# Two jobs on raw x: a row factor applied at PSUM eviction, and a second, normed operand built beside it

## The chip, the cores and the metric

One core of a Trainium2 chip runs the whole computation in one launch. The metric is device microseconds of that launch. Three runs of the kernel before took 1221.35, 1222.22 and 1223.20 us; the median is 1222.22 us. The engines are named as in the profile: PE (TensorE), DVE (VectorE), ACT (ScalarE), POOL (GpSimd) and SP, which issues DMAs.

## The reference, cut to what matters

Two layers of a block work on 256 tokens of 1024 channels, all in float32. What the change touches is the first norm of layer 0 and the first products behind it:

```python
def rmsnorm(x, g):
    y = x * lax.rsqrt(jnp.mean(x * x, axis=-1, keepdims=True) + EPS)
    return y * g

h = rmsnorm(x, ln_mix_pre[l])
proj = h @ w_in[l]
xr, yr, q, kv, g_nsa, qm, g_merge = jnp.split(proj, IN_OFFSETS, axis=-1)
o_a = rglru_branch(xr, yr, ...)               # xr through a convolution and a scan, yr through a gelu
o_b = nsa_branch(q, kv, g_nsa, ...)
o_c = memory_branch(qm, mem, ln_mem[l], w_mem_kv[l])   # rmsnorm(mem) @ w_mem_kv for keys and values
```

The norm has two factors: a gain per channel (g) and one number per token, the rsqrt, called the row factor here. Since it is the same for all channels of a token, `(x * g) @ w` times the row factor is the same as `h @ w`.

## The kernel before, in words

**Tiling.** Every weight matrix is cut into units of 512 KB (256 contraction rows by 512 columns as a rule). A unit is loaded into `raw` (a ring of NRAW = 5 buffers, `dma_unit`, line 334, on SP's queue), and split by `split_unit` (line 342) into a high part `whi` (ACT, a copy that rounds to fp32r) and a low part `wlo` (DVE, raw minus whi); these have rings of NSPL = 4 buffers. The operand is kept channel-major in the same two parts (`XT`, line 363: `hTh` and `hTl`, four quarters of 256 channels by 256 tokens each). Each product of two fp32 matrices is three matmuls: high by high, low by high and high by low. A job of four units (`wstat_job`, line 582) takes 96 matmuls of 256 columns into two PSUM banks.

**Order.** The jobs are issued in the order of the string ORDER0 (line 166): xr1, xr0, yr0, yr1, then vm0 (values of the memory branch), km0, and so on. `run` (line 643) issues them step by step, one step for each unit; the units are numbered u0, u1, ... here (xr1 is u0 to u3, xr0 u4 to u7, yr0 u8 to u11, yr1 u12 to u15, vm0 u16 to u19). At the top of a step it issues the splits of one or two later units, as far as `may_split` allows; then it asks `drain` for the pieces of the operand that this unit needs; then it issues the products, and after each 128 contraction rows calls `side`.

**Side work.** All that is not products lives in lanes: generators that name the engine of their next few instructions, "A", "D", "G" or "P1" (PE, with one PSUM bank to take). While the program is traced, a planner (`Order`, line 73, and `Meter`, line 106) keeps an estimated clock for every engine. `side` (line 252) goes over the lanes in the order of their priority, and within one priority in the order in which they were spawned, and issues a step if it would hold no engine up:

```python
elif r > max(od.T[e], now) + TOL or od.T[e] > now + HORIZON:   # TOL 0.07, HORIZON 3.0 us, now = od.T["P"]
    break
```

`drain` and `bank` (which waits until a PSUM bank is counted as free) call `step` (line 272) instead: it issues the step that can start first by the estimate, and of those that are within 0.3 us of each other the first in the list of lanes. The planner fixes nothing but the order; on the chip each engine then executes its instructions in that order, waiting on semaphores. The estimated PE clock knows when a unit's split is ready and which lanes are done, but a lane is done when it has been issued.

**The start.** SP loads x in four tiles (two token tiles by two halves of 512 channels), the gain as a row, and five weight units. PE runs 16 matmuls that nothing reads. `first_norm` (line 431): per token tile, ACT sums the squares of both halves, POOL adds EPS and raises to -0.5, DVE multiplies both halves by the row factor (`hn`); then per quarter PE transposes four 128x128 pieces into a PSUM bank (`tr`), ACT writes the high part with the gain as a scale per partition, and DVE the low part. Job xr1 starts with its first quarter.

At the first step `start` (line 1788) also loads the recurrent branch's gate weights, the memory's gains and the four tiles of `mem` (SP), small parameters and tables (13 DMAs on POOL's queue), and spawns in this order: the norm of `mem`, the lane `prm` (28 small DVE instructions on the recurrent parameters) and the lane `const` (the rotary tables, some 27 small DVE instructions). The norm of `mem` spawns its four half tiles (`half_lane`, line 480: DVE `hn`, PE transposes, ACT `mTh`, DVE `mTl`) only once its row factor is there, so behind prm and const in the list. vm0 needs them.

**PSUM.** Four banks tagged "mm" for products, four tagged "at" for side work. xr1's results are copied to `xs` by ACT (`xr_epi`, line 1348), which frees its two banks.

Of the kernel before, what the change touches and what calls it, by code (L numbers as in the profile page):

```python
# [11 lines left out]
F32 = mybir.dt.float32  # L12
# [60 lines left out]
class Order:  # L73
    """Estimated engine clocks, by which the issue order of independent work is chosen while it is traced."""
# [31 lines left out]
class Meter:  # L106
    """An engine whose instructions are counted on its estimated clock."""
# [38 lines left out]
def trunk_kernel(ctx, tc, x, mem, positions, ln_mix_pre, w_in, conv_w, conv_b, lru_wr, lru_br, lru_wi, lru_bi,  # L146
# [79 lines left out]
    def start_of(ln):  # L226
        """When the next instructions of this lane could start, or None while it waits for others."""
# [14 lines left out]
        if e == "V":  # L242
            ln.alt = e = min("AD", key=lambda k: max(od.T[k], ln.r + od.lat(ln, k)) + VBIAS * (k == "D"))
        r = ln.r + od.lat(ln, e)
        if len(n) > 1:
            k = int(n[1])
            if len(banks_free["at"]) < k:
                return None, e
            r = max(r, banks_free["at"][k - 1])
        return r, e  # L250

    def side():
        """Issue what can go without holding an engine up."""
# [18 lines left out]
    def step(prio=9):  # L272
        """Issues the side work of at most this priority that can start first."""
# [26 lines left out]
    def copy(dst, src):  # L300
        """On the engine that a "V" step chose."""
# [86 lines left out]
    def half_sumsq(src):  # L388
        """Sum of (src / 32)^2, a part of the mean over 1024 channels."""
# [11 lines left out]
    def first_half(src):  # L401
        """Starts the mean square of a token tile with its first half."""
# [10 lines left out]
    warm, gcol = [], []  # L413

    def load_column(g):
        """A gain as a column for every 128 channels."""
# [14 lines left out]
    def first_norm(o):  # L431
        """The first norm of x, by 256 channels of all tokens, its gain applied after the transposes."""
        hn = {}

        def scale(t):
            yield "A"
            el, box = first_half(xt[t][0])
            s1 = half_sumsq(xt[t][1])
            yield el
            yield "G"  # L440
            r = rstd_of(box[0], s1)
            for h in range(2):
                yield "D"
                hn[t, h] = a([P, 512], F32, "hn")
                dve.tensor_scalar(hn[t, h], xt[t][h], r, None, op0=OP.mult)

        def quarter(q):
            while len(hn) < NT * 2 and not all((t, q // 2) in hn for t in range(NT)):
                yield scaled
            yield "P1"  # L450
            pt = bank([P, 2, S], "at", "tr")
            for t in range(NT):
                for i in range(2):
                    c = 2 * (q % 2) + i
                    pe.transpose(pt[:, i, t * P:(t + 1) * P], hn[t, q // 2][:, c * P:(c + 1) * P], ident)
# [10 lines left out]
            for i in range(2):  # L466
                dve.scalar_tensor_tensor(o.lo[q][:, i, :], pt[:, i, :], col[i], f(o.hi[q][:, i, :]),
                                         op0=OP.mult, op1=OP.subtract)
            free()

        scaled = [spawn(scale(t), prio=0) for t in range(NT)]
        for q in range(4):
            spawn(quarter(q), f"first{q}", prio=0)

    def busy(n):
        """Products that nothing reads, to keep the tensor engine's clock up where it would wait."""
# [3 lines left out]
    def half_lane(src, r, gt, t, h, o):  # L480
        """Half a token tile, normed and transposed into channel-major parts."""
# [17 lines left out]
    def norm_lane(src, t, gt, o, name, sums=None):  # L499
        """rmsnorm of one token tile, transposed into o; the halves' lanes are name + tile + half."""  # L500
# [122 lines left out]
    def weave(js):  # L623
        """Jobs whose units take turns."""
# [18 lines left out]
    def run(jobs):  # L643
# [15 lines left out]
        def may_split(m, n):  # L659
            """Whether unit m may be split at step n."""  # L660
# [11 lines left out]
        while nd < NRAW:  # L672
            dma_unit(us[nd], 0.0)
            nd += 1
        warm.append(bank([P, 2 * P], "mm", "warm"))
# [39 lines left out]
    def epilogue(fn):  # L715
        """What follows a job's products, as urgent side work that gives its PSUM banks back."""
# [66 lines left out]
    def rope_mul(src, nh, s, t1, t2, rows=P):  # L783
        """The products of a rotation of src [rows, nh*64] in PSUM."""
# [115 lines left out]
    def gelu_lane(y, s):  # L900
        """s = 2 * gelu(y)"""
# [101 lines left out]
    def blocks_lane(l, j, g2, gx):  # L1003
        """Overlapping token blocks with their positional embedding, as contraction rows (token pair, channel)."""
# [117 lines left out]
    def kprep_lane(w, kd, res):  # L1122
        """Transposed keys of two groups times -1/8: high and low parts, each on both partition halves."""
# [17 lines left out]
    def qprep_lane(t, g, st, qs):  # L1141
        """Transposed queries of four heads: the high part on one partition half, the low part on the other."""
# [119 lines left out]
    def value_lane(l, t, g, scores, cxl, cx, ptl, st, o, before):  # L1262
        """One query tile of one group: transposed probabilities times values, all branches in one bank."""
# [16 lines left out]
        def mul(ps, vx):  # L1280
            """Rows 64*par.. of heads of parity par take the products with the high part, the other rows the low part's."""
# [34 lines left out]
    def nsa_lane(l, st, gt, o):  # L1316
        """st: q[t, g], k[g] = (hi, lo), v[br, t] = (hi, lo), c = compressed keys and values."""
# [23 lines left out]
    def layer(l):  # L1341
# [5 lines left out]
        # recurrent branch  # L1347
        def xr_epi(half):
            def go(banks):
                E["xs", half] = [a([P, 2, S], F32, "xs") for _ in range(2)]  # L1350
                yield "A"
                for b in range(2):
                    act.activation(E["xs", half][b], banks[b], AF.Copy)
# [26 lines left out]
        for half in range(2):  # L1380
            need = normed(f"bnd{l - 1}b") if l else lambda u, t: [f"first{u}"]
            J[f"xr{half}"] = wstat_job(win, 0, C_XR + 512 * half, HX, xr_epi(half), pre=pre_xr(half), unit_need=need)
            J[f"yr{half}"] = wstat_job(win, 0, C_YR + 512 * half, HX, yr_epi(half))

        # memory branch
# [31 lines left out]
        # merge  # L1417
# [414 lines left out]
```

## Time and profile before

| | us |
|---|---|
| median of three runs | 1222.22 |
| span of the profiled execution, first to last instruction | 1221.4 |
| PE busy in it | 1205.7 (99%) |
| DVE busy | 900.5 (74%) |
| ACT busy | 737.0 (60%) |
| first product of xr1 | 13.82 |
| first product of vm0 | 64.04 |

The profiled execution has no time of its own beside its span; the median lies 0.8 us above that span, which is what lies around the first and the last instruction. A matmul's end is modelled, so the distance between the starts of two matmuls is what one costs. A high part of a weight unit takes ACT about 1 us, a low part DVE 1.15 us, its 24 products take PE 2.9 us.

### The profile page before, as it was taken

The numbers are of one execution on the slowest core, as the hardware profiler recorded it, in microseconds if no ns is written. First come the engines' busy times: TensorE is split into PE (matmuls) and PEld (weight loads), VectorE is DVE, ScalarE is ACT, GpSimd is POOL, SyncE is SP. The second block draws the span as 40 slices with busy tenths as digits, with TensorE's granted clock in tenths as the row PEclk, the third lists the DMA queues.
The fourth block names the chain that finished last, engine by engine and source line by source line (L and its number), as shares of the span: only waits on it lengthen the run. The fifth ranks groups of instructions, "written<-read, shape, count | busy, mean of one in ns | idle before, by whom it ended". The sixth has DMA issues, their size and how long they took to land.

```text
span 1221.4 us, 21789 instructions
## 1 busy us (share of the span) xinstructions
PE 1205.7 (99%) x8491; PEld 1128.1 (92%) x8491; DVE 900.5 (74%) x1503; ACT 737.0 (60%) x1327; POOL 37.6 (3%) x88
## 2 busy tenths in 40 slices
PE   8999999999999999999999999999999999999997
PEld 7999988999999999998989999999999997899896
DVE  4979898968898676555567587998878867655555
ACT  5676856767666465444455688676556655645443
POOL 4000000000000020000001000000000001000000
PEclk8999999999999999999999999999999999999999
DMA  8656656644353766666657566585444356566661
GB/s 286 202 157 183 183 161 196 189 138 128 115 177 126 239 189 187 196 185 186 206 172 218 146 180 174 150 257 153 138 123 133 110 157 238 163 187 186 190 190 68
DMA packets 121271, 212.71 MB, mean 174 GB/s; under 512 B 10441, under 2 KB 24098, under 8 KB 121169
## 3 DMA queue, kind: packets, MB, share of 16 engines
q1 hardware_dynamic: 120752, 211.19, 57.0%
q8 instruction: 66, 1.08, 0.4%
q0 software_dynamic: 416, 0.15, 0.1%
q14 instruction: 37, 0.30, 0.1%
HBM read 208.16 MB, written 1.05 MB: 171 GB/s over the span
## 4 chain that ended last, share of the span: by engine, by line
PE 93%; ACT 2%; DMA 2%; DVE 2%; issue 1%; SPq 0%; POOL 0%; POOLq 0%; DVEq 0%; ACTq 0%
PE mm L140 63%; PE acc L140 14%; PE sc L140 3%; PE ob L140 2%; PE wo L140 2%; PE pt L140 2%; PE hid L140 1%; PE gp L140 1%; PE mo L140 1%; PE msc L140 1%; PE tr L140 1%; DMA mem<-in_mem_dram 1%; PE csc L140 1%; ACT junk L140 1%; DMA raw<-in_mlp_w_dram 0%
## 5 line engine op out<-in xcount | busy, mean ns | idle before, releaser
L140 DVE TENSOR_TENSOR wlo<-raw,whi 128x1024 fp32r<-128x1024 f32 (+1 forms) x371 | 447.0, 1214 | 225.3 <-ACT whi L140 224.0
L140 ACT ACTIVATE whi<-raw 128x1024 fp32r<-128x1024 f32 (+1 forms) x371 | 385.7, 1056 | 205.3 <-PE mm L140 118.8
L140 PE MATMUL mm<-hTh,whi 128*128 128x256 f32 x832 | 240.1, 289 | 0.0
L140 PE MATMUL mm<-hTh,wlo 128*128 128x256 f32 x832 | 235.8, 283 | 0.0
L140 PE MATMUL mm<-hTl,whi 128*128 128x256 f32 x832 | 235.7, 283 | 0.0
L140 PEld LDWEIGHTS mm<-hTh,whi 128*128 128x128 f32 x832 | 159.7, 192 | 1.4
L140 PEld LDWEIGHTS mm<-hTl,whi 128*128 128x128 f32 x832 | 159.8, 192 | 0.3
L140 PEld LDWEIGHTS mm<-hTh,wlo 128*128 128x128 f32 x832 | 159.8, 192 | 0.0
L140 PE MATMUL mm<-hmh,whi 128*128 128x256 f32 x480 | 135.8, 283 | 0.0
L140 PE MATMUL mm<-hmh,wlo 128*128 128x256 f32 x480 | 135.8, 283 | 0.0
L140 PE MATMUL mm<-hml,whi 128*128 128x256 f32 x480 | 135.8, 283 | 0.0
L140 PE MATMUL acc<-whi,rh 128*128 128x512 f32 x256 | 99.8, 390 | 0.0
L140 PE MATMUL acc<-wlo,rh 128*128 128x512 f32 x256 | 99.8, 390 | 0.0
L140 PE MATMUL acc<-whi,rl 128*128 128x512 f32 x256 | 99.6, 389 | 0.0
L140 PEld LDWEIGHTS mm<-hml,whi 128*128 128x128 f32 x480 | 92.1, 192 | 0.5
L140 PEld LDWEIGHTS mm<-hmh,whi 128*128 128x128 f32 x480 | 92.1, 192 | 0.5
L140 PEld LDWEIGHTS mm<-hmh,wlo 128*128 128x128 f32 x480 | 92.1, 192 | 0.0
L140 ACT ACTIVATE pr<-sc,mx 128x256 f32<-128x256 f32 (+1 forms) x128 | 52.0, 426 | 27.8 <-DVE mx L140 27.7
L140 PEld LDWEIGHTS acc<-whi,rl 128*128 128x128 f32 x256 | 48.1, 188 | 10.2
L140 PEld LDWEIGHTS acc<-wlo,rh 128*128 128x128 f32 x256 | 48.1, 188 | 9.5
L140 PEld LDWEIGHTS acc<-whi,rh 128*128 128x128 f32 x256 | 48.1, 188 | 9.5
L140 PE MATMUL mm<-whi,hTh 128*128 128x512 f32 x128 | 50.5, 394 | 0.0
(310 smaller groups left out, 2584.9 us busy)
## 6 DMA issues: line engine op xcount, KB each, us to landing
raw<-in_w_in_dram SPq DMA_DIRECT2D x136, 512.0 KB, 3.8
raw<-in_mlp_w_dram SPq DMA_DIRECT2D x128, 512.0 KB, 4.3
raw<-in_w_mem_kv_dram SPq DMA_DIRECT2D x32, 512.0 KB, 4.2
raw<-in_cmp_w_dram SPq DMA_DIRECT2D x16, 512.0 KB, 4.0
raw<-in_w_br_rnn_dram SPq DMA_DIRECT2D x16, 512.0 KB, 3.7
raw<-in_w_br_mem_dram SPq DMA_DIRECT2D x16, 512.0 KB, 3.7
raw<-in_w_br_nsa_dram SPq DMA_DIRECT2D x16, 512.0 KB, 3.7
raw<-in_w_out_dram SPq DMA_DIRECT2D x16, 512.0 KB, 4.6
```

The lines of the kernel that those rows point to most:

```text
L140: return fn(*args, **kw)
```

## The change

The diff also drops all docstrings and comments. Its core:

```diff
@@ the start: order of the loads
-    def load_x(t):
-        for h in range(2):
+    def load_x(h):
+        for t in range(NT):
             nc.sync.dma_start(out=xt[t][h], ...)
+        dma_clock[0] += 2 * 0.73
+    dma_clock[0] = 2.0
     load_x(0)
     column = load_column(ln_mix_pre[0:1, :])
-    load_x(1)
-    dma_clock[0] = 2.4 + 4 * 0.73
...
-    first_norm(env[0]["X"])
+    first_operands(env[0]["X0"], env[0]["X"])
-    run(order)
+    run(order, lambda: load_x(1))          # called behind the DMA of the first weight unit
@@ def first_operands(o, on), in place of first_norm(o)
+        ones = a([P, P], F32, "ones")
+        pool.memset(ones, 1.0)
         def quarter(q):
-            ...                             # waited for hn
             yield "P1"
-            pt = bank([P, 2, S], "at", "tr")
+            pts[q] = pt = bank([P, 2, S], "at", "tr")
-                    pe.transpose(pt[...], hn[t, q // 2][:, c * P:(c + 1) * P], ident)
+                    pe.transpose(pt[...], xt[t][q // 2][:, c * P:(c + 1) * P], ident)
             ...                             # high part (ACT, gain as scale), low part (DVE): as before
-            free()
+        def scale(t):
+            ...                             # sums of squares (ACT), rstd (POOL): as before
+            yield "D"
+            diag[t] = a([P, P], F32, "diag")
+            dve.tensor_scalar(diag[t], ident, r, None, op0=OP.mult)
+        def spread():
+            yield [spawn(scale(t)) for t in range(NT)]
+            yield "M1"                      # PE, with one "mm" bank
+            pt = bank([P, NT, P], "mm", "rs")
+            for t in range(NT):
+                pe.matmul(pt[:, t, :], ones, diag[t], start=True, stop=True)
+            rows.append(a([P, S], F32, "rows"))
+            yield "D"
+            dve.tensor_copy(rows[0], pt.rearrange("p t c -> p (t c)"))
+            free("mm")
+        def normed_quarter(q):
+            yield f"@first{q}"
+            yield "@rows"
+            n = a([P, 2, S], F32, "xn")
+            yield "D"
+            for i in range(2):
+                dve.scalar_tensor_tensor(n[:, i, :], pts[q][:, i, :], gcol[0][:, 2 * q + i:2 * q + i + 1], rows[0],
+                                         op0=OP.mult, op1=OP.mult)
             free()
+            yield "A"
+            act.activation(on.hi[q], n, AF.Copy)
+            yield "D"
+            dve.tensor_tensor(on.lo[q], n, f(on.hi[q]), op=OP.subtract)
         for q in range(4):
+            od.cur.r = 5.0 if q < 2 else 8.2
             spawn(quarter(q), f"first{q}", prio=0)
+        spawn(spread(), "rows", prio=0.2, child=0.2)
+        for q in range(4):
+            spawn(normed_quarter(q), f"norm{q}", prio=0.3)
@@ xr_epi, layer 0
+                    yield "@rows"
+                    yield "D"
+                    for b in range(2):
+                        dve.tensor_tensor(E["xs", half][b], banks[b], bc(rows[0], ...), op=OP.mult)
-                yield "A": act.activation(E["xs", half][b], banks[b], AF.Copy)     (kept for layer 1)
@@ jobs of layer 0
-            J[f"xr{half}"] = wstat_job(win, 0, C_XR + 512 * half, HX, ...)
+            J[f"xr{half}"] = wstat_job(win, 0, C_XR + 512 * half, lambda: E["X0"], ...)
+            need = None if l else lambda u, t: [f"norm{u}"]
             J[f"yr{half}"] = wstat_job(win, 0, C_YR + 512 * half, HX, yr_epi(half), unit_need=need)
```

So xr1 and xr0 multiply x times gain (operand X0, tiles xTh and xTl). The row factors of all tokens are laid out along the free axis on every partition (`rows`, from a product of a matrix of ones with two diagonal matrices), xr's results are multiplied by them on the way out of PSUM, and the normed operand X for all later jobs is built from the same transposes, whose four "at" banks are held until then. `start_of` learns the step "M1".

## Rows read from the trace of the kernel before

**Rows 1.** The page, part 1: busy us, share of the span, instructions.
```profile
PE 1205.7 (99%) x8491; PEld 1128.1 (92%) x8491; DVE 900.5 (74%) x1503; ACT 737.0 (60%) x1327; POOL 37.6 (3%) x88
```
**Rows 2.** Waits of PE, whole span: waiter, releaser: us in total, times, longest.
```profile
PE tr L140 <- DVE hn L140: 5.6, 5, 2.8
```
**Rows 3.** Timeline of the first 20 us: start, duration, engine, line, operation, count, [idle before].
```profile
2.48 3.49 PEld L140 LDWEIGHTS warm<-dmask,identr 128*128 128x128 f32 x16 [2.48 <-DVE dmask L140]
...
7.09 0.44 PE L140 MATMUL tr<-ident,hn 128*128 128x128 f32 x2 [0.67 <-DVE hn L140]
8.06 0.63 ACT L140 ACTIVATE junk<-xt 128x512 bf16<-128x512 f32 x1 [1.11 <-DMA xt<-in_x_dram]
...
11.08 0.84 ACT L140 ACTIVATE hTh<-tr,gcol 128x256 fp32r<-128x256 f32 x2 [2.29 <-PE tr L140]
...
11.95 0.88 DVE L140 SCALAR_TENSOR_TENSOR hTl<-tr,gcol,hTh 128x256 fp32r<-128x256 f32 x2 [1.26 <-ACT hTh L140]
...
12.74 2.42 DVE L140 TENSOR_TENSOR wlo<-raw,whi 128x512 fp32r<-128x512 f32 x3
...
13.82 0.41 PE L140 MATMUL mm<-hTh,whi 128*128 128x256 f32 x1
...
17.08 0.28 PE L140 MATMUL mm<-hTh,whi 128*128 128x256 f32 x1
```
**Rows 4.** DMA issues of 2.9 to 3.2 us, then of 3.2 to 3.6: us to landing (median).
```profile
raw<-in_w_in_dram SPq DMA_DIRECT2D x1, 512.0 KB, 6.4
xt<-in_x_dram SPq DMA_DIRECT2D x1, 256.0 KB, 5.5
...
raw<-in_w_in_dram SPq DMA_DIRECT2D x2, 512.0 KB, 6.8
```
**Rows 5.** Windows, PE alone: stretch, us, busy (count), granted clock, DMA share, GB/s.
```profile
9.50:9.80 0.30, 0.00 (x0) 0.67 1.06 410
...
16.30:16.60 0.30, 0.30 (x4) 0.79 1.02 389
```
**Rows 6.** Timeline of ACT, 17 to 31 us.
```profile
17.77 2.95 ACT L140 ACTIVATE whi<-raw 128x1024 fp32r<-128x1024 f32 x3
...
26.71 0.63 ACT L140 ACTIVATE junk<-mem 128x512 bf16<-128x512 f32 x1 [4.19 <-DMA mem<-in_mem_dram]
...
29.37 1.06 ACT L140 ACTIVATE xs<-mm 128x512 f32<-128x512 f32 x2
```
**Rows 7.** Timeline of DVE, 17 to 83 us.
```profile
18.86 3.50 DVE L140 TENSOR_TENSOR wlo<-raw,whi 128x1024 fp32r<-128x1024 f32 x3
...
78.88 0.69 DVE L140 TENSOR_TENSOR ml<-mm,mh 128x512 fp32r<-128x512 f32 x1 [1.24 <-ACT mh L140]
```
**Rows 8.** Timeline of SP, the issue of DMAs.
```profile
3.00 12.56 SPq L338 DMA_DIRECT2D raw<-in_w_in_dram  x7
...
17.98 4.01 SPq L1752 DMA_DIRECT2D mem<-in_mem_dram  x4
```
**Rows 9.** Timeline of PE: the seventh product of xr0, the first of vm0.
```profile
27.86 0.28 PE L140 MATMUL mm<-hTh,whi 128*128 128x256 f32 x1
...
64.04 0.40 PE L140 MATMUL mm<-whi,mTh 128*128 128x512 f32 x1
```
**Rows 10.** Timeline of DVE, 42 to 62 us: prm, half tiles of mem, const.
```profile
42.51 0.18 DVE L140 TENSOR_SCALAR sp<-sp 128x16 f32<-128x16 f32 x1
42.72 0.17 DVE L140 TENSOR_TENSOR sp<-sp,sp 128x16 f32<-128x16 f32 x1
...
44.94 1.41 DVE L140 TENSOR_TENSOR mTl<-tr,mTh 128x256 fp32r<-128x256 f32 x4
...
52.75 1.13 DVE L140 SCALAR_TENSOR_TENSOR ang<-rnd,ang 128x96 f32<-128x96 f32 x4
...
60.01 1.08 DVE L140 TENSOR_TENSOR mTl<-tr,mTh 128x256 fp32r<-128x256 f32 x3
```
**Rows 11.** Windows, all engines: stretch, us, busy of PE, PEld, DVE, ACT, POOL.
```profile
25.00:30.00 5.00, 5.00 (x44) 5.00 (x43) 0.00 (x0) 3.29 (x10) 1.51 (x6) 1.00 1.05 387
```

More of the change, by code (lines that the diff above doesn't have):

```diff
@@ L243, in start_of @@
             ln.alt = e = min("AD", key=lambda k: max(od.T[k], ln.r + od.lat(ln, k)) + VBIAS * (k == "D"))
+        tag = "at"
+        if e == "M":
+            e, tag = "P", "mm"
         r = ln.r + od.lat(ln, e)
@@ L246, in start_of @@
             k = int(n[1])
-            if len(banks_free["at"]) < k:
+            if len(banks_free[tag]) < k:
                 return None, e
-            r = max(r, banks_free["at"][k - 1])
+            r = max(r, banks_free[tag][k - 1])
         return r, e
@@ L411, in rstd_of @@
         return r
-    warm, gcol = [], []
+    warm, gcol, rows = [], [], []
     def load_column(g):
@@ L429, in load_column, with first_operands @@
         return lane()
[L431 to L441, printed above, removed]
-            for h in range(2):
-                yield "D"
-                hn[t, h] = a([P, 512], F32, "hn")
-                dve.tensor_scalar(hn[t, h], xt[t][h], r, None, op0=OP.mult)
+    def first_operands(o, on):
+        ones = a([P, P], F32, "ones")
+        pool.memset(ones, 1.0)
+        pts = {}
         def quarter(q):
-            while len(hn) < NT * 2 and not all((t, q // 2) in hn for t in range(NT)):
-                yield scaled
             yield "P1"
-            pt = bank([P, 2, S], "at", "tr")
+            pts[q] = pt = bank([P, 2, S], "at", "tr")
             for t in range(NT):
@@ L454, in quarter @@
                     c = 2 * (q % 2) + i
-                    pe.transpose(pt[:, i, t * P:(t + 1) * P], hn[t, q // 2][:, c * P:(c + 1) * P], ident)
+                    pe.transpose(pt[:, i, t * P:(t + 1) * P], xt[t][q // 2][:, c * P:(c + 1) * P], ident)
             busy(BUSY)
@@ L468, in quarter @@
                                          op0=OP.mult, op1=OP.subtract)
-            free()
-        scaled = [spawn(scale(t), prio=0) for t in range(NT)]
+        def scale(t):
+            yield "A"
+            el, box = first_half(xt[t][0])
+            s1 = half_sumsq(xt[t][1])
+            yield el
+            yield "G"
+            r = rstd_of(box[0], s1)
+            yield "D"
[19 more added lines that the diff above has]
+                                         op0=OP.mult, op1=OP.mult)
+            free()
+            yield "A"
+            act.activation(on.hi[q], n, AF.Copy)
+            yield "D"
+            dve.tensor_tensor(on.lo[q], n, f(on.hi[q]), op=OP.subtract)
+        diag = {}
         for q in range(4):
+            od.cur.r = 5.0 if q < 2 else 8.2
             spawn(quarter(q), f"first{q}", prio=0)
+        spawn(spread(), "rows", prio=0.2, child=0.2)
+        for q in range(4):
+            spawn(normed_quarter(q), f"norm{q}", prio=0.3)
     def busy(n):
@@ L641, in weave, with run @@
         return Job([js[n].units[i] for _, n, i in turns], lambda: None, mm, unit_need=unit_need)
-    def run(jobs):
+    def run(jobs, between):
         us, flat = [], []
@@ L674, in run @@
             nd += 1
+            if nd == 1:
+                between()
         warm.append(bank([P, 2 * P], "mm", "warm"))
@@ L1350, in go @@
                 E["xs", half] = [a([P, 2, S], F32, "xs") for _ in range(2)]
-                yield "A"
-                for b in range(2):
-                    act.activation(E["xs", half][b], banks[b], AF.Copy)
+                if l == 0:
+                    yield "@rows"
+                    yield "D"
+                    for b in range(2):
+                        dve.tensor_tensor(E["xs", half][b], banks[b], bc(rows[0], "p (o s) -> p o s", [P, 2, S]), op=OP.mult)
+                else:
+                    yield "A"
+                    for b in range(2):
+                        act.activation(E["xs", half][b], banks[b], AF.Copy)
                 free("mm", 2)
@@ L1381, in layer @@
             need = normed(f"bnd{l - 1}b") if l else lambda u, t: [f"first{u}"]
-            J[f"xr{half}"] = wstat_job(win, 0, C_XR + 512 * half, HX, xr_epi(half), pre=pre_xr(half), unit_need=need)
-            J[f"yr{half}"] = wstat_job(win, 0, C_YR + 512 * half, HX, yr_epi(half))
+            J[f"xr{half}"] = wstat_job(win, 0, C_XR + 512 * half, (lambda: E["X"]) if l else (lambda: E["X0"]), xr_epi(half),
+                                       pre=pre_xr(half), unit_need=need)
+            need = None if l else lambda u, t: [f"norm{u}"]
+            J[f"yr{half}"] = wstat_job(win, 0, C_YR + 512 * half, HX, yr_epi(half), unit_need=need)
         def m_epi(rnd, key):
@@ L1757, in mem_prep @@
         spawn(norm_both(ms, gm, env[l]["M"], f"mnorm{l}"))
-    def load_x(t):
-        for h in range(2):
+    def load_x(h):
+        for t in range(NT):
             nc.sync.dma_start(out=xt[t][h], in_=x[0, t * P:(t + 1) * P, 512 * h:512 * h + 512])
+        dma_clock[0] += 2 * 0.73
+    dma_clock[0] = 2.0
     load_x(0)
     column = load_column(ln_mix_pre[0:1, :])
-    load_x(1)
-    dma_clock[0] = 2.4 + 4 * 0.73
     for l in range(DEPTH):
@@ L1781, in trunk_kernel @@
                 u.early = True
-    env[0]["X"] = XT("hT")
+    env[0]["X0"], env[0]["X"] = XT("xT"), XT("hT")
     od.cur.r = 4.5
     spawn(column, "gcol", prio=0)
-    first_norm(env[0]["X"])
+    first_operands(env[0]["X0"], env[0]["X"])
     first_pre = order[0].pre
```

## The prediction

> **What bounds the kernel now.** The page's first part comes first: PE is busy for 99% of the span [rows 1], so the time moves only if products start earlier or wait more. The waits of PE come second: nearly all it waits for after its first instruction is `hn`, 5.6 us, of which the longest, 2.8 us, lies in the start [rows 2]. The timeline of the start shows why. The last tile of x lands at 8.0, its sum of squares and POOL's power follow, transposes end 11.0, the high part takes ACT 0.84, the low part DVE 0.88, the first `wlo` comes behind them, and xr1's first product stands at 13.82 [rows 3]. PE meanwhile lost its clock: the granted clock falls at about 9.6, some 2 us after the transposes that ended at 7.5, and is back at about 16.4 [rows 3, 5]; the first 12 products cost 0.21 us each and not 0.12. So 13.82 us is what the change can attack. Two more readings decide: what ACT and DVE do up to 64 us, and in which order, since both execute in the order that the planner wrote.
>
> **Part 1, the start (removes).** The first quarter no longer needs the row factor, only x's first halves, which are now the first two loads. PE's 16 matmuls end at 6.0 [rows 3], the gain column and four transposes follow to 7.0, the high part to 7.85, the low part to 8.7. The first weight unit takes the place of x's third and fourth tile, so it lands where the fourth did, 2.53 + 5.5 = 8.0 and not 3.0 + 6.4 = 9.4 [rows 4]; its first high part ends 8.6, the first `wlo` (0.6 of a group of 2.42) at 9.4. First products at 8.7, steady from 9.4: 4.4 us earlier than 13.82. PE has been idle for under 2 us, so I keep the high clock: 12 × 0.09 = 1.1 us more. x's second halves land at 9.4; the transposes of quarters 2 and 3 stand behind 12 products (10.6) and wait for nothing; were they 1.4 us late, as much as the loads were swapped by, PE would wait 0.2. The transposes themselves cost the same on x as on hn. POOL's 13 DMA issues now stand ahead of the powers; the sums they follow end after 15 anyway.
>
> **Part 2, quarter 2 (adds a wait).** Going through the planner's conditions with its own costs: at the side call in u0's step the row-factor lanes (priority 0.2) put four sums of squares on ACT ahead of quarters 2 and 3. By the estimate those high parts end at 14.3 and 14.9, their low parts could start on DVE at 14.4 while DVE's clock stands at 12.6, so they are left; the next step's splits of u2 and u3 take DVE to 18.3, over 3 us ahead of PE, and the low parts are issued behind them. On the chip: the second weight unit lands at about 10.6 (the median 6.8 of two [rows 4]), `whi` of u1 ends 11.7, quarter 1 12.4, four sums at 0.67 15.1 (from 26.71 to 29.37 [rows 6]), quarters 2 and 3 16.6, `whi` of u2 17.6, of u3 18.6; DVE then `wlo` u2 to 18.8 and u3 to 20.0 (1.15 each [rows 7]), and the first low part of quarter 2 at 20.4 (0.44 [rows 3]). PE ends u1 at 16.3 and waits about 4 us. Before, u2 began at 17.08 + 36 × 0.12 = 21.4, so 1 us of the lead is left.
>
> The clock in this wait. Before, an idle stretch of about 2 us cost the high clock [rows 3, 5]; 4 us should too. Twelve products at 0.21 were lost time of 1.1 us then; 12 to 28 now are 1.1 to 2.5. The Trainium skill (TensorE: Matmul & The Clock Gate, "HAM oscillation") says that the half rate is the default and that every wait for data long enough throttles PE anew, so that products after it start cold. The rows bear out one such fall. By that rule PE alone would reach the mark of part 3 at 28.5 to 29.9, without it at 27.4; since part 3's own wait ends at 29.8, what the rule moves is the 1.0 us for the clock in part 4: without it the forecast would be 1227.4.
>
> **Part 3, xr0's second bank (adds a wait).** Take the seventh product of xr0, at 27.86 before [rows 9], as the mark. Banks tagged "mm": one is the warm-up's, two xr1's, the fourth now holds the spread row factors (`rs`) until DVE copies them. xr0 needs two, and gets only the warm-up's; so `bank` steps until the copy is issued. But the top of that step has by then issued u6's split, and the side call before it the sums over `mem`. So DVE's copy stands behind `wlo` of u6, that behind `whi` of u6 on ACT, that behind four sums that wait for mem. Behind the waiting ACT instruction are queued all later high parts, behind DVE's the copy and xr1's eviction, and PE waits for the copy. Mem landed at 26.7 [rows 6]; SP issued it from 17.98, after two raw loads that waited for the low parts of u0 and u1 [rows 8]. Those end 2.3 us earlier now (12.9 for 15.2), and the same bytes follow, so mem comes at about 24.4 (23.4 to 25.4). Then 2.66 for the sums, 1.0 `whi`, 1.2 `wlo`, 0.4 the copy (between 0.35, a 128x256 read of PSUM in the group of four [rows 10], and 0.44 [rows 3]), and handovers: 29.8. Two fp32 products of the ones are nowhere in the trace; below, a transpose (0.2 each [rows 3]), above, the longest matmul (0.4 [rows 9]); 0.5 for both, hidden beside this wait. Mark at 29.9: **2.0 us behind** before.
>
> **Part 4, vm0's operand (moves).** DVE did nothing from 25 to 30 [rows 11]; it still waits for mem then, and afterwards has more to do. Already before, prm and const kept the half tiles of mem waiting: four `mTl` come only after prm, three only after const, at 61.1, 2.9 us before vm0 [rows 9, 10]. Before, the half tiles' `hn` were in DVE's queue ahead of prm; now DVE's estimated clock stands at its limit of 3 us ahead of PE through xr0, yr0 and yr1, each allowance goes to evictions and normed quarters, then to prm, then const, all earlier in the list, and the four `hn` are issued only by vm0's drain, behind the rest of const. DVE from 29.8 on:
>
> - evictions of xr1 and xr0, 4 × 0.65 (128x512 from PSUM: 0.69 [rows 7]) = 2.6
> - normed quarters: 8 × 0.42 = 3.4 [rows 3], 4 subtractions × 0.62 = 2.5
> - `wlo` of u7 to u18: 12 × 1.15 = 13.8
> - prm 28 × 0.21 = 5.9, const 27 × 0.25 to 0.28 = 6.8 [rows 10]
> - the wait for xr0's end (its eviction stands before `wlo` of u10): 1.5
>
> Sum 36.5: 66.3. Three `hn` (128x512, 0.69 each), transposes and the first ACT copy: vm0's products run from about 69.3. PE wants to start vm0 at 29.9 + 282 × 0.12 + 0.3 = 64.0 and idles 2 us or more until the transposes; another low-clock stretch, at vm0's start, 0 to 2 us, taken at 1.0. The end moves by 69.3 − 64.04 + 1.0 = **6.2**. The bounds: DVE's list is good to 1.5 us either way, mem's landing to 1, the clock to 1; if the half tiles get in before const, 6.8 less, and part 3 alone remains. Behind vm0 DVE lags in the recurrent branch's work, which no job reads for many units; I take 0 (0 to 2 if it delays a `wlo`). The eight more tiles of X0 and four of xn lie in a ring of 66 buffers that the first jobs don't fill: 0.
>
> Sum: span 1221.4 + 6.2 = 1227.6, with the 0.8 around it by the median 1228.4 us.
>
> **The rivals.**
> (a) The lead holds. Were low parts and copy ahead of the weights' on DVE, PE would keep the 4.4 + 1.1 less 0.5 for the added products: 1217.2. For it: PE bounds, and DVE's empty 25 to 30 could take the new work. Against: the order above, which doesn't hang on a close call except the copy's (0.13 us of estimate). Chance 0.10.
> (b) Only part 3 holds, vm0's operand comes in time: 1222.2 + 2.0 = 1224.2. For it: 2.9 us of slack before. Against: the list of 36.5 us. It decides where `hn` is issued before const. Chance 0.20.
> (c) Forecast, parts 3 and 4: 1228.4. Chance 0.55.
> (d) More: const and the recurrent branch's instructions push vm0's second half tiles too, and the low clock lasts: 3 to 5 us more, about 1232.5. Chance 0.15.
>
> **How the numbers follow.** A measurement of this kernel can tell 0.2%, 2.4 us, from no change. (a) is faster, (b) lies within, (c) and most of (d) are slower: 0.10, 0.20, 0.70. Range: (c) with its bounds is 1225 to 1231; it reaches down to cover most of (b) and up to the lower part of (d): 1222.5 to 1232.
>
> **What would show it.** xr1's first product near 9; PE idle from about 16 to 20 with DVE's `xTl` as releaser; the copy into `rows` behind a `wlo` that waits for ACT's sums over mem, and xr0's products into its second bank near 30; `mTl` after the last of const, and vm0's first product near 69. I am wrong if PE runs through from 9 to 64 without these waits, or if vm0 starts before 66.

## The result, and the profile after

The changed kernel took 1231.57 us (median of 4, 1231.26 to 1233.36), the kernel before beside it 1221.86 us: ratio 1.0074, 95% interval 1.0059 to 1.0088. Slower, as forecast (1228.4 us, 1222.5 to 1232.0), by 9.7 us where the prediction had 6.2. The profiled execution is 1231.78 us with a span of 1230.1; the span grew by 8.7. (The text ahead of the prediction puts 0.8 us outside the span; that is a median less the span of one execution. Where time and span of one execution are both on record, 1.7 to 1.9 us lie outside it for either kernel.)

TensorE's row of the page, and its waits up to 240 us (waiter, releaser: us in total, times, longest); they answer to [rows 1] and [rows 2]:
```profile
PE 1208.7 (98%) x8495; PEld 1129.5 (92%) x8495; DVE 908.5 (74%) x1518; ACT 738.3 (60%) x1327; POOL 37.0 (3%) x89
```
```profile
PE mm L140 <- DVE xTl L140: 2.9, 1, 2.9
PE mm L140 <- DVE wlo L140: 2.8, 3, 1.7
PE warm L140 <- DVE dmask L140: 2.5, 1, 2.5
PE tr L140 <- DVE hn L140: 1.9, 1, 1.9
PE gp L140 <- DVE xc L140: 1.0, 1, 1.0
PE mm L140 <- ACT whi L140: 0.7, 1, 0.7
```
The `hn` waits of the start are gone, and others have come, nearly all on VectorE. The longest, in the timelines of ACT, PE and DVE up to 30 us (start, duration, engine, operation, count, [idle before]; they answer to [rows 3, 6, 7]):
```profile
6.75 1.28 ACT L140 ACT_TABLE_LOAD   x1 [6.75 <-DVE gcol L140]
8.05 0.84 ACT L140 ACTIVATE xTh<-tr,gcol 128x256 fp32r<-128x256 f32 x2
...
22.59 0.63 ACT L140 ACTIVATE junk<-mem 128x512 bf16<-128x512 f32 x1 [2.79 <-DMA mem<-in_mem_dram]
```
```profile
20.60 0.38 PE L140 MATMUL mm<-xTl,whi 128*128 128x256 f32 x1 [2.90 <-DVE xTl L140]
...
27.80 0.61 PE L140 MATMUL rs<-diag,ones 128*128 128x128 f32 x4
...
28.96 0.35 PE L140 MATMUL mm<-xTh,whi 128*128 128x256 f32 x1
```
```profile
17.00 2.36 DVE L140 TENSOR_TENSOR wlo<-raw,whi 128x1024 fp32r<-128x1024 f32 x2 [3.56 <-ACT whi L140]
19.28 1.65 DVE L140 SCALAR_TENSOR_TENSOR xTl<-tr,gcol,xTh 128x256 fp32r<-128x256 f32 x4
...
26.33 1.23 DVE L140 TENSOR_TENSOR wlo<-raw,whi 128x1024 fp32r<-128x1024 f32 x1 [2.74 <-ACT whi L140]
28.45 0.42 DVE L140 COPY rows<-rs 128x256 f32<-128x256 f32 x1 [0.90 <-PE rs L140]
```
Quarter 2's low part stands behind two `wlo`, TensorE is idle to 20.60, and xr0's seventh product (28.96; 27.86 in [rows 9]) is 1.1 us late although the first product came 4.4 us earlier. Around vm0, DVE and PE:
```profile
64.15 0.21 DVE L140 TENSOR_SCALAR ang<-ang 128x96 f32<-128x96 f32 x1
64.27 2.07 DVE L140 SCALAR_TENSOR_TENSOR hn<-mem,rstd,gain 128x512 f32<-128x512 f32 x3
```
```profile
65.08 2.44 PE L140 MATMUL tr<-ident,hn 128*128 128x128 f32 x12 [1.85 <-DVE hn L140]
67.17 0.77 PE L140 MATMUL mm<-whi,mTh 128*128 128x512 f32 x1
...
75.84 0.67 PE L140 MATMUL gp<-xc,gw 128*128 128x256 f32 x2 [0.99 <-DVE xc L140]
...
134.06 0.38 PE L140 MATMUL mm<-mTh,wlo 128*128 128x256 f32 x1 [1.71 <-DVE wlo L140]
```
`hn` follows the last constant; vm0 starts at 67.17 (64.04 in [rows 9]). The granted clock fell about 1 us behind the end of each of the two waits (windows: stretch, us, busy (count), clock, DMA, GB/s; they answer to [rows 5]):
```profile
21.80:25.00 3.20, 3.20 (x17) 0.50 1.05 389
...
66.00:69.50 3.50, 3.50 (x14) 0.51 0.01 4
```

One table serves all that follows: when TensorE issued its first weight product, vm0's first, and the first of the compressed scores (`csc`); the us between these two; and the span. From `csc` to the end every kernel took 988.0 to 989.1 us.

| kernel | first | vm0 | csc | csc − vm0 | span |
|---|---|---|---|---|---|
| before | 13.82 | 64.04 | 233.42 | 169.4 | 1221.4 |
| changed | 9.46 | 67.17 | 241.78 | 174.6 | 1230.1 |
| e4_clock | 9.46 | 68.61 | 243.22 | 174.6 | 1231.8 |
| a_noxn | 9.46 | 67.41 | 241.86 | 174.5 | 1230.0 |
| a_xspool | 9.46 | 69.31 | 243.86 | 174.6 | 1232.1 |
| e3_mem_later | 9.46 | 66.48 | 241.03 | 174.6 | 1229.4 |
| e1_mem_first | 9.46 | 65.05 | 243.07 | 178.0 | 1231.7 |
| e5_prm_mem | 9.39 | 66.24 | 243.40 | 177.2 | 1231.8 |
| e2_low_first | 9.15 | 59.33 | 235.66 | 176.3 | 1224.6 |
| c12 | 9.46 | 60.11 | 230.01 | 169.9 | 1218.3 |
| c12t | 8.76 | 59.79 | 229.34 | 169.6 | 1218.4 |
| c_xspool | 8.46 | 61.45 | 234.64 | 173.2 | 1223.7 |
| b_load | 11.65 | 73.43 | 242.81 | 169.4 | 1230.9 |
| b_spread | 10.73 | 65.34 | 239.55 | 174.2 | 1228.4 |

Of the changed kernel's 8.7 us, 3.1 stand at vm0, 5.2 between vm0 and `csc`, and 0.3 behind.

### The profile page after: what moved, and what is told of

Same layout as the page of the kernel before. It is cut to its first block, busy times and chain, and to the rows that moved or that the text cites. A ratio compares the mean times of both kernels' runs of the same rounds, so it can differ in the third digit from the quotient of the medians.

```text
span 1230.1 us, 21818 instructions
## 1 busy us (share of the span) xinstructions
PE 1208.7 (98%) x8495; PEld 1129.5 (92%) x8495; DVE 908.5 (74%) x1518; ACT 738.3 (60%) x1327; POOL 37.0 (3%) x89
## 4 chain that ended last, share of the span: by engine, by line
PE 91%; DVE 3%; ACT 2%; DMA 1%; issue 1%; POOL 0%; SPq 0%; DVEq 0%; POOLq 0%; ACTq 0%
PE mm L140 61%; PE acc L140 14%; PE sc L140 3%; PE ob L140 2%; PE wo L140 2%; PE pt L140 2%; PE hid L140 1%; PE mo L140 1%; PE gp L140 1%; DMA raw<-in_mlp_w_dram 1%; PE tr L140 1%; PE msc L140 1%; DVE wlo L140 1%; ACT whi L140 1%; PE csc L140 1%
## 5 line engine op out<-in xcount | busy, mean ns | idle before, releaser
L140 PE MATMUL mm<-hTh,whi 128*128 128x256 f32 x768 | 221.7, 289 | 0.0
L140 PE MATMUL mm<-hTh,wlo 128*128 128x256 f32 x768 | 217.4, 283 | 0.6 <-DVE wlo L140 0.6
L140 PE MATMUL mm<-hTl,whi 128*128 128x256 f32 x768 | 217.2, 283 | 0.0
L140 PEld LDWEIGHTS mm<-hTh,whi 128*128 128x128 f32 x768 | 146.9, 191 | 1.4
L140 PEld LDWEIGHTS mm<-hTh,wlo 128*128 128x128 f32 x768 | 146.9, 191 | 0.9 <-DVE wlo L140 0.8
L140 PEld LDWEIGHTS mm<-hTl,whi 128*128 128x128 f32 x768 | 147.0, 191 | 0.3
```

Source lines behind the costliest of these rows:

```text
L140: return fn(*args, **kw)
```

## The experiments

The theory at the outset: the order costs the time (low parts, copy and half tiles of mem stand behind other work), and each misplacement that is mended pays its wait back. The rival: VectorE's added work has to be paid whatever the order.

**Half tiles of mem ahead (e1_mem_first).**
```
-        spawn(norm_both(ms, gm, env[l]["M"], f"mnorm{l}"))
+        spawn(norm_both(ms, gm, env[l]["M"], f"mnorm{l}", 1 if l else 0.35))
```


> Layer 0's half tiles of mem get a higher priority (0.35 for 1), so that their products of mem and gain (hn) are issued on VectorE ahead of the parameter and constant work; no work is added or left out, and the start stays as in the changed kernel (quarter 2's low part late, the spread copy behind wlo of u6). Theory of order: the wait of 1.85 us before the transposes of the first half tile and the low clock behind it (about 1.6 us) come from hn standing behind the constants. Then vm0's first product stands near 65.1 (64.04 before, 67.17 in the changed kernel), vm0 starts at the high clock, and the end comes 3 to 4 us earlier: about 1227.5 us. Rival, theory of load: VectorE is full from 28 to 66 us whatever the order, so that the work displaced (parameters, constants) makes the recurrent branch's xc late instead; then the waits for xc grow by what hn gives back and the time stays at 1230 to 1232 us.

Measured: 1233.09 us, ratio to before 1.0086 (1.0073 to 1.0100). vm0 started at 65.05, as the theory had it, without a wait and at full clock; and nothing was gained. The new wait stands elsewhere (timelines of PE, DVE and SP, 105 to 150 us):
```profile
130.50 0.58 PE L140 MATMUL mm<-mTh,wlo 128*128 128x256 f32 x1 [4.63 <-DVE wlo L140]
```
```profile
127.37 0.35 DVE L140 TENSOR_TENSOR gs<-g,pet 128x120 f32<-128x120 f32 x1 [5.55 <-DMA g<-kcs]
128.44 0.87 DVE L140 TENSOR_TENSOR gs<-g,pet 128x120 f32<-128x120 f32 x3 [0.71 <-DMA g<-kcs]
129.23 1.21 DVE L140 TENSOR_TENSOR wlo<-raw,whi 128x1024 fp32r<-128x1024 f32 x1
```
```profile
110.32 11.84 SPq L341 DMA_DIRECT2D raw<-in_w_mem_kv_dram  x4
122.25 0.50 SPq L1522 DMA_DIRECT2D g<-kcs  x1
```
`kcs` was written by 117.6, but its DMA to `g` stood in SP's queue behind the issue of four weight loads that took 11.84 us; VectorE's `gs` waited for that DMA, the `wlo` behind `gs`, and TensorE for the `wlo`. Both theories missed it: the rival's time (1230 to 1232) was 1.1 us short, and not through the gates' xc, for which nothing waited here.

**Parameters, then mem, then constants (e5_prm_mem).**
```
+        spawn(norm_both(ms, gm, env[l]["M"], f"mnorm{l}", 1 if l else 0.35))
+        spawn(prm_lane(prows), "prm", prio=0.33)
```


> The changed kernel with another order of priorities alone: parameters first, then the half tiles of mem, then the constants (in the run with mem first the parameters came last of the two and the gates' xc went behind; there TensorE lost 4.6 us at 126 us to wlo behind a gs that waited 5.5 us for a DMA). Theory of place: hn in time and xc not pushed, so vm0's first product at about 65 us, no wait for hn, smaller waits for xc: 1225 to 1228 us. Rival: VectorE's list between 28 and 100 us is as long as before and the order only picks who waits: 1230 to 1233 us.

Measured: 1232.70 us, 1.0081 (1.0064 to 1.0098), with `wlo` waited for 4.8 us at one place and the loads of weights ahead of `g` for 11.84 us again. So which of the two goes first doesn't matter; with the late start hn in time is worth nothing in either.

**Sums of squares behind quarter 3 (e2_low_first).**
```
         def scale(t):
+            yield "@first3"
             yield "A"
```


> One line is added: a token tile's sums of squares wait in the planner until quarter 3 has been issued. That puts the high and low parts of quarters 2 and 3 ahead of the splits of u2 and u3, and the copy of the spread row factors ahead of wlo of u6 and of the sums over mem; no work is added or left out. Theory of order: the idle 2.9 us for quarter 2's low part and its low clock go, xr0's seventh product comes at about 23.6 us (27.86 before, 28.96 in the changed kernel), VectorE starts its list some 4 us earlier, hn of mem is no longer late, and the lead of about 4 us lasts to the end: about 1218 us, faster than the kernel before. Rival, theory of load: the added VectorE work (about 8 us of normed quarters, copy and subtractions) must be paid before vm0 and the gates in any order; the lead is taken back as a wait at vm0 or at the gates, and the time is 1225 to 1230 us.

Measured: 1226.06 us, 1.0030 (1.0018 to 1.0043): 5.5 us better than the changed kernel, still slower than before. The idle 2.9 us went, TensorE was at full clock from its first product on, vm0 came at 59.33, 4.7 us ahead of before. Then 6.9 us more than before were lost up to `csc`, 4.8 of them in short waits (`wlo` 2.0 us in 3, `mTl` 1.3, `vx` 1.1, hn 0.4). The theory of order is right for the start and wrong for the end; the rival, theory of load, had the time (1225 to 1230) and the lead taken back behind vm0's start.

**Both edits (c12).** The lines of e1 and e2 together.

> Both edits of order together: the sums of squares of the token tiles wait for quarter 3, and the half tiles of mem go ahead of parameters and constants. Theory of order: the lead of the start (4.4 us and the 1.1 us for the clock, less 0.5 for the added products) lasts: 1217 to 1218 us, at most 1 us from the first edit alone, since that alone already lifts hn ahead of most of the parameter work. Rival, theory of load: 1225 us or more, with waits for the gates' xc in place of those for hn.

Measured: 1220.69 us (11 runs) beside 1222.64, ratio 0.9984 (0.9975 to 0.9993): faster than both kernels, though than the one before by less than the 0.2% set in the prediction. It lies between the two theories' bands. Apart from the 2.5 us at the very start, no wait for VectorE over 0.5 us is left up to 240 us:
```profile
PE warm L140 <- DVE dmask L140: 2.5, 1, 2.5
PE mm L140 <- DVE wlo L140: 0.5, 1, 0.5
PE mm L140 <- ACT whi L140: 0.4, 1, 0.4
PE mm L140 <- DVE vx L140: 0.3, 1, 0.3
```
The edit that gave nothing alone gives 5.4 us here: the two don't add. Where mem went first with the late start, vm0 was followed by 178.0 us; here, with the same work in another order on TensorE and VectorE, by 169.9. SP issues its DMAs in the same order in both runs; here `gs` waited 0.82 us for `g`, there 5.55.

**The low clock at vm0 (e4_clock).**
```
+        if o is env[0].get("M") and (t, h) == (0, 0):
+            for i in range(16):
+                pe.eng.matmul(pt[:, 0:2, :], identr, dmask, start=True, stop=True)
         for i in range(4):
             pe.transpose(pt[:, i, :], hn[:, i * P:(i + 1) * P], ident)
```


> The changed kernel with 16 products that nothing reads (128x256, ahead of the transposes of the first half tile of mem), in the stretch of 1.85 us in which TensorE waits for hn; every other instruction keeps its place. Theory: the first products of vm0 run at 0.43 us and not 0.22 because the engine stood idle, which costs about 1.6 us; with the wait filled the granted clock stays at 1.00 there and the end comes 1.0 to 2.0 us earlier: 1229.5 to 1230.5 us. Rival: the clock is low there for another reason, or the slow products only fill a time in which later operands would be waited for anyway (gates, wlo); then the time stays within 0.5 us of the changed kernel's 1231.6.

Measured: 1233.01 us, 1.0087 (1.0073 to 1.0101). The clock was held:
```profile
66.00:69.50 3.50, 3.48 (x24) 1.00 0.38 136
```
and nothing came of it (1.4 us above the changed kernel, outside both bands). From the spread products (`rs`, 29.59; 27.80 in the changed kernel, whose start was quicker) to vm0 it took 39.0 us instead of 39.4; then the gates waited 1.6 us for xc instead of 1.0. Up to `csc` TensorE waited 4.0 us for 3.3 and was 0.7 us quicker with its products: vm0's slow products had filled a time that was waited for anyway.

**VectorE without xn (a_noxn).**
```
-                dve.scalar_tensor_tensor(n[:, i, :], pts[q][:, i, :], ..., rows[0], ...)
+            nc.gpsimd.memset(n, 0.5)
+                od.note("D", ...)
```


> The changed kernel, every engine's order as it is, without VectorE's eight products of quarter, gain and row factor (xn, 8 x 0.47 us); the tile that they fill is set to a constant by POOL, so the normed operand's values are left out. Theory of load (VectorE has more to do between 28 and 78 us than it has time for): what VectorE loses TensorE gets back, hn of mem comes 3.3 us earlier, the wait of 1.9 us and its low clock go, the waits for xc and wlo behind it shrink, and the time falls by 3 to 5 us to 1227 to 1228.5 us. Rival, theory of place: the late instructions wait for a DMA, for ScalarE or for the planner's place whatever VectorE's load, so that the wait only moves and the time stays within 1 us of 1231.6.

Measured: 1232.43 us, 1.0087 (1.0072 to 1.0101): no gain. VectorE did 3.3 us less, and `hn` still started at 64.88:
```profile
40.00 1.41 DVE L140 TENSOR_TENSOR xs<-mm,rows 128x512 f32<-128x512 f32 x2 [2.94 <-PE mm L140]
```
Its queue came to xr0's eviction, which the change moved from ScalarE to VectorE, and stood there 2.94 us until TensorE had ended xr0. In the changed kernel that wait is 1.47 us, and the eviction starts at 39.40; what is saved ahead of it is waited there. From this eviction to `hn` it took 24.9 us in both kernels. So VectorE's list of instructions before vm0 is dated from the end of xr0, not from the copy. In this run the clock stayed at 1.00 from 64 to 72 us, with the same wait of 1.85 us, and `csc` was the same.

**xr's eviction off VectorE (a_xspool).**
```
-                    yield "@rows"
-                    yield "D"
-                        dve.tensor_tensor(E["xs", half][b], banks[b], bc(rows[0], ...), op=OP.mult)
+                    yield "A"
+                        act.activation(raw[b], banks[b], AF.Copy)
+                    free("mm", 2)
+                    yield "@rows"
+                    yield "G"
+                        pool.tensor_tensor(E["xs", half][b], raw[b], bc(rows[0], ...), op=OP.mult)
```


> The changed kernel; the results of xr1 and xr0 leave PSUM as plain copies on ScalarE (as before the change), and POOL multiplies them by the row factors from SBUF. Nothing is left out. VectorE loses its four products of 0.69 us and, with them, the place in its queue at 38.6 us where it waits 1.5 us for xr0's last product; half tiles of mem stay behind the constants. Theory of the queue (what stands behind xr0's eviction on VectorE is dated from xr0's end, so that eight fewer xn gave nothing): hn comes about 4 us earlier (60 for 64.3), the wait of 1.9 us goes, xc comes earlier too and the waits for xc and wlo behind vm0 (3.3 us) shrink: 1224.5 to 1227.5 us. Rival: the next wlo waits for ScalarE and so for TensorE in its place, and takes the time up as in the run without xn: over 1230 us.

Measured: 1233.34 us, 1.0083 (1.0067 to 1.0100); `hn` at 66.42. VectorE's list, from the copy (32.41) to `hn`, ran without the wait for xr0, in 34.0 us for 35.8. It should have been 4.3 shorter (1.5 and 2.8), but POOL's products slowed it:
```profile
34.44 2.17 DVE L140 TENSOR_TENSOR wlo<-raw,whi 128x1024 fp32r<-128x1024 f32 x1
...
43.09 0.96 DVE L140 TENSOR_SCALAR hb<-pcol 128x32 f32<-128x32 f32 x1
43.97 0.16 DVE L140 TENSOR_SCALAR sp<-pcol 128x16 f32<-128x16 f32 x1
44.16 1.15 DVE L140 TENSOR_TENSOR sp<-sp,pcol 128x16 f32<-128x16 f32 x1
```
```profile
32.97 2.56 POOL L140 TENSOR_TENSOR xs<-xu,rows 128x512 f32<-128x512 f32 x2 [6.14 <-DVE rows L140]
41.71 3.57 POOL L140 TENSOR_TENSOR xs<-xu,rows 128x512 f32<-128x512 f32 x2 [6.18 <-ACT xu L140]
```
2.17 for 1.21, 0.96 for 0.18 and 1.15 for 0.17: 2.7 us given back. And the copy itself came 4 us later than in the changed kernel: it stands behind `wlo` of u6 in both, but `whi` of u6 now stood behind ScalarE's copies of xr1, which waited 3.12 us for TensorE. The run can't tell the theory from its rival cleanly; what it shows is that this way out costs as much as it saves.

**Sums over mem later (e3_mem_later, one run).**
```
-        od.cur.r = max(od.cur.r, dma_clock[0] + 2.0)
+        od.cur.r = max(od.cur.r, dma_clock[0] + 2.0) + (0 if l else 4.0)
```


> The changed kernel with layer 0's sums over mem allowed 4 us later in the planner, so that whi of u6 stands ahead of them on ScalarE; quarter 2's low part stays late. If the sums over mem price xr0's start, as the prediction's third part has it, TensorE's wait of 0.7 us for whi goes and xr0's seventh product comes 0.7 to 1.5 us earlier than 28.96. Rival: TensorE's own late restart at 20.6 us prices it, and the product stays within 0.3 us. hn of mem stays behind the constants either way, so the time is 1230 to 1232 us in both.

Measured: 1231.38 us. `whi` of u6 now stood ahead of the sums, and waited 5.06 us for TensorE to give a buffer back; xr0's seventh product came at 29.16. The rival holds: TensorE's own restart prices that mark, the sums over mem don't. (The wait of 0.7 us for `whi` that the theory counted on stands at 9.46, ahead of the first product, and not at xr0's start: from 20.60 to 28.96 the changed kernel's TensorE waits for nothing.)
```profile
25.04 1.06 ACT L140 ACTIVATE whi<-raw 128x1024 fp32r<-128x1024 f32 x1 [5.06 <-PE mm L140]
26.01 0.61 ACT L140 ACTIVATE junk<-mem 128x512 bf16<-128x512 f32 x1
```

**The added work on the kernel before (b_load, b_spread).**
```
+            for _ in range(k):   # k by unit: b_load u6 to u9 4, 4, 3, 3; b_spread u10 to u16 2 each
+                nc.vector.tensor_tensor(scr, xt[0][0], xt[0][1], op=OP.subtract)
```


> The kernel before, every engine's order as it is, with 14 subtractions of 128x512 that nothing reads on VectorE behind wlo of u6 to u9 (4, 4, 3, 3; about 0.65 us each, 9.1 us in all): the size of the work that the change adds to VectorE, without any of the change's start. Theory of load: VectorE stood idle for 4.9 us between 28 and 64 us, so that some 4 us are left over; vm0 or the gates wait for them and the time rises by 3 to 6 us. Rival: the cost of the change lies in the late low part of quarter 2 and in the order, and the added work finds room: less than 1.5 us.

> The kernel before, every engine's order as it is, with the same 14 subtractions of 128x512 that nothing reads, now two behind each wlo of u10 to u16 (42 to 61 us), behind the half tiles' hn. In this stretch VectorE of the kernel before shows no idle time, and its last mTl ends 2.9 us before vm0. Theory of the list (each us added there moves everything behind it, and 2.9 us of it are slack): vm0 about 6 us later, 1227.5 to 1229.5 us. Rival (wlo run ahead of TensorE by the ring of buffers, so that added work is caught up): under 2.5 us.

Measured: b_load 1232.63 us, 1.0085 (1.0071 to 1.0100); b_spread 1230.20 us, 1.0056 (1.0038 to 1.0075). Both cost more than either theory gave: 10 us for 10.0 us of work (14 × 0.71), and 8. In b_load four stand ahead of the first two hn in VectorE's queue and four ahead of the other two, and TensorE has mem's transposes in its own queue there:
```profile
33.01 2.86 DVE L363 TENSOR_TENSOR scr<-xt,xt 128x512 f32<-128x512 f32 x4
35.79 0.74 DVE L140 SCALAR_TENSOR_TENSOR hn<-mem,rstd,gain 128x512 f32<-128x512 f32 x1
```
```profile
36.58 1.12 PE L140 MATMUL tr<-ident,hn 128*128 128x128 f32 x4 [6.00 <-DVE hn L140]
```
All of it is lost at vm0 (9.4), nothing behind (169.4). b_spread is the reverse: vm0 only 1.3 later, 4.8 lost behind it (2.6 more in waits, 2.2 in slow products behind the longest of them). The order on every queue is that of the kernel before in both; what differs is how far VectorE is when TensorE starts vm0. The first xc for the gates starts 3.0 us ahead of vm0's first product in the kernel before, 2.4 ahead in b_load, and 3.3 behind in b_spread (2.4 behind in the changed kernel). The lines are of before, b_spread and b_spread:
```profile
61.00 1.51 DVE L140 SCALAR_TENSOR_TENSOR xc<-xs,pcol,xc 128x255 f32<-128x255 f32 x3
```
```profile
68.67 1.51 DVE L140 SCALAR_TENSOR_TENSOR xc<-xs,pcol,xc 128x255 f32<-128x255 f32 x3
```
```profile
71.38 0.50 PE L140 MATMUL mm<-wlo,mTh 128*128 128x512 f32 x1 [1.99 <-DVE wlo L140]
```
Two of the subtractions added in b_spread, 1.4 us, run behind vm0's start. So VectorE of the kernel before had no room for 10.0 us of work in either place; the changed kernel's VectorE is busy 8.0 us more (908.5 for 900.5).

**The table load, and the version with it (c12t, c_xspool).** In c12t, one line on c12; c_xspool is c12t with the edit of a_xspool.
```
+    early = cp.tile([P, 1], F32, name="early")
+    nc.scalar.activation(early, mhalf, AF.Copy)
```


> The kernel with both edits of order, and one more: a 128x1 copy on ScalarE at the start, whose only use is that the table load of 1.28 us, which stood behind the gain column at 6.75 us, comes before it. Theory: the first high part stands behind the table load, so the first product comes 0.8 to 1.3 us earlier (8.2 to 8.7 for 9.46), and the end about 1 us: 1219.7 for 1220.7 us. Rival: the first weight unit's landing and its split set the steady start, or VectorE's list sets vm0 anyway; then the first product moves and the time does not.

> The version with both edits of order and the early table load, with xr's results through ScalarE and POOL as in the first of these runs. If VectorE's list is still what limits the lead behind xr0, the end comes 0.5 to 1.5 us earlier than the 1220.8 us of that version; if not (no wait for VectorE stands in its trace from 30 to 120 us), it stays within 0.7 us of it.

Measured: c12t 1220.80 us, 0.9987 (0.9978 to 0.9996). The table load went to 0.79, the first product came at 8.76 and `csc` 0.7 us earlier; the time is that of c12. c_xspool 1223.74 us, 1.0007 (0.9997 to 1.0017): 2.9 us worse than c12t, where the forecast was better or the same, with 4.1 us of waits for `wlo` behind the start. c12 and c12t are the versions to keep; they can't be told apart.

## Why the prediction came out as it did

The direction and the cause (in-order queues on VectorE, as the planner wrote them) were right, and the time lies 3.2 us above the forecast. That is above forecast (c)'s own bounds (1225 to 1231) and where rival (d) stood (3 to 5 us more), but not by (d)'s mechanism: the fourth half tile's `hn` did come only behind vm0's start (68.91), but no wait of 0.3 us for it shows in the changed kernel, and the low clock's price was nil. That the range still held the time is in part luck, since two terms were too large and a third was missing. Of its signs one didn't come as said: vm0 at 67.17, not near 69. By its steps:

- **Part 1.** First products at 9.46 and not 8.7, steady from 10.45 and not 9.4: the table load, at 0.79 us before the change, now stands behind the gain column, at 6.75, for 1.28 us (0.7 of the 0.76 us, by c12t). That was not seen. The clock was at its high level from the first product, as said.
- **Part 2.** Right: TensorE waited for quarter 2's low part until 20.60 (20.4 forecast), 2.9 us and not 4 since it came there later, and the clock stood at 0.50 until 25. e2_low_first, which mends it and also puts the copy of part 3 ahead, shows that the start is worth the most: 5.5 us alone, 10.9 with mem's order.
- **Part 3.** The order came as walked, copy behind `wlo` of u6 behind the sums over mem, but it priced nothing: mem landed at 22.59, not 24.4, and VectorE waited 0.90 for TensorE's `rs`, not TensorE for it. The mark was 1.1 us late, not 2.0, all of it from part 2 (e3_mem_later).
- **Part 4.** Right in kind: hn behind the last constant, at 64.27. The list was put at 36.5 us from 29.8 and took 35.4 from 28.87, so vm0 came 3.1 us late and not 5.2. The term of 1.5 for xr0's end was in the sum; that work saved ahead of it therefore brings `hn` no earlier (a_noxn) was not seen.
- **The clock, 1.0.** It fell at vm0 to 0.51, but its price was nil (e4_clock, a_noxn). The Trainium skill (TensorE: Matmul & The Clock Gate, "HAM oscillation") has every wait that is long enough throttle the engine anew. The rows at vm0 don't settle whether 1.85 us is long enough: that wait was followed by 0.51 in the changed kernel and by 1.00 in a_noxn. In neither did it change the end.
- **Behind vm0, 0 to 2.** The step that failed. It cost 5.2 us. Its ground was that no job reads the recurrent branch's work for many units; TensorE's gates (`gp`) come 7.1 us after vm0's first product, and waited for xc. Five kernels with the changed kernel's order on every queue from vm0 on lost 5.2 to within 0.2, though their vm0 lay anywhere from 66.5 to 69.3, with the low clock or without: it isn't how late vm0 is. In all five xc also starts 2.4 to 2.6 us behind vm0's first product, and b_spread lost 4.8 in the order of the kernel before, with xc 3.3 behind. So VectorE's lag at vm0 can cost nearly as much by itself. The order counts too: c12, where the gates come 16.7 us after vm0's first product, lost only 0.5 with xc 5.5 behind. How much of the 5.2 is the lag and how much the changed kernel's order, no run separates. Named in the trace are the gates' xc (1.0 to 1.6 us), and `wlo`, 0.6 and 1.3 to 1.7; that last stands behind `gs`, which waited 3.1 us for the DMA of `kcs`. In the changed kernel 1.9 us of the 5.2 are no wait: about 1 is vm0's slow products (the first six start 67.17 to 69.45), 0.4 the fourth half tile's transposes, which stood ahead of vm0 before; for the rest there is only the other order. What makes the planner write that order was not tried.
```profile
72.42 0.60 PE L140 MATMUL tr<-ident,hn 128*128 128x128 f32 x4
```

Measured, 3.1 + 0 + 5.2 against 5.2 + 1.0 + 0: two terms too large, one missed. Behind `csc` another 0.3 was lost, and the 0.8 us that the sum adds outside the span is 1.7 in the changed kernel's profiled execution: the profiled execution of before, with a span of 1221.4, was longer than most (the median span of the other runs is 1220.6 to 1220.9). Rival (a), the lead holds, put at 1217.2 if the low parts and the copy went first: with the order mended (c12) 1220.69. vm0 was then 3.9 us ahead, not 5.0, and the start of the kernel before was less of a loss than its profile shows. In b_load and b_spread, the same instructions up to there, x's last tile was read at 6.7 and 6.6 and not 8.06 [rows 3], and the first product stood at 11.65 and 10.73; b_spread then waited 2.1 us for hn of mem, up to 31.8, where the kernel before waited 0.2: half of its earlier start (1.6 of 3.1 us) was given back there.

## What to carry to other kernels

Ask of an edit that shifts a written order not only which wait it removes, but which instructions change places on each in-order queue, SP's among them, until the old order is met again: here the two kernels' orders differ up to about 190 us, and the stretch behind vm0 cost more than the start did. Ask too how far each engine lags behind the one that bounds: in b_spread the old order with a lag cost 4.8 us. Work saved ahead of an instruction that waits for another engine is worth nothing behind it, and an edit that gives nothing alone can give 5 us with another. Before a lead is priced from one profile, look at a second one: the landing of the first loads moved the start by 3 us.

## What the runs showed of the hardware

- POOL products of 128x512 in SBUF slowed some of VectorE's instructions beside them: `wlo` 2.17 for 1.21 us, two of 128x16 and 128x32 about 1 us for 0.17 (a_xspool), two `hn` 3.46 for 1.41 (c_xspool). Others beside them kept their time (`sp` 0.16 at 43.97), and the second POOL pair took 3.57 us for 2.56. The last slowed one ended with POOL's pair (45.31, 45.28). The Trainium skill (GPSIMD Engine Reference, "Specifications") says that POOL's SBUF interfaces are shared with VectorE, with contention for instructions with two SBUF inputs or in a 2-port mode; this agrees for `wlo` and the slow `sp`, and for `hb`, which has one tensor input, no row shows the mode.
- Where ScalarE's table load stands depends on its first instruction: at 0.79 us where that waited for a load of x (before) or for POOL (c12t), at 6.75 where it waited for VectorE's gain column.
- A wait of 1.85 us on TensorE was followed by the low clock in one run (0.51 from 66 to 69.5) and not in another (1.00).
